# A search in place of a cyclic weight buffer, and all convolutions ahead of mixer B, in a two-layer conv/gMLP decoder step

## Chip, cores, metric

One Trainium2 chip, 8 cores. Each core runs the same program on one sequence of 2,048 rows and 16 sample rows. The metric is the device time of the slowest of the 8 cores, in microseconds. Some executions of any kernel on this chip fall into a slower state (one die at a lower granted clock, 1,483 to 1,730 us here); they are left out everywhere, and only fast runs are compared.

Names: PE is the TensorE matmul unit, DVE the VectorE, ACT the ScalarE, POOL the GpSimd engine (it issues all weight loads), SP the SyncE (it issues the other transfers).

## The reference, cut to what matters

Two layers; each is three token mixers side by side on one input projection, an output projection, and a SwiGLU FFN.

```python
def mixer(h, ...):
    z = h @ w_in
    a_val, a_gate, b_x, b_b, b_c, c_u, c_v = jnp.split(z, SPLITS, axis=-1)
    # A: GLU -> causal depthwise conv (31) -> LayerNorm over channels -> silu
    hist_a = jnp.concatenate([buf_a, a_val * jax.nn.sigmoid(a_gate)], axis=1)
    ya = jax.nn.silu(layernorm(causal_dwconv(hist_a, dw_a) + dw_a_bias, ln_a_g, ln_a_b))
    # B: b_b * conv_w3(b_c * b_x)
    yb = b_b * causal_dwconv(jnp.concatenate([buf_b, b_c * b_x], axis=1), conv_b_w)
    # C: u * (W_s_masked @ LN(v) + b), in chunks of 128 rows
    yc = jax.nn.gelu(c_u) * chunk_spatial(layernorm(jax.nn.gelu(c_v), ...), w_s, b_s)
    return jnp.concatenate([ya, yb, yc], axis=-1) @ w_o
# x += mixer(rmsnorm(x));  x += (silu(gate) * up) @ w_ffn_out;  two layers, one final norm
```

## The kernel before

The kernel records every operation as a node, and a list scheduler, run ahead of time, decides the order of each engine's queue. A node gets a due time, worked backwards from everything that waits for it, loads included. On each engine the ready node with the earliest due time goes next. And PE may run work up to 60 us ahead of the order in which the program states it.

```python
def place(self):
    for nd in reversed(nodes):
        d = nd.T if nd.e == "pe" else INF          # T: PE time before it in program order
        lat = 2000.0 + nd.nbytes / 200.0 if nd.nbytes else LAT
        for s, off in nd.succ:
            d = min(d, s.due + off - nd.cost - lat)
        # ... (cut)
    # ... take the engine that can start first; among its ready nodes:
            for nd in cand[e]:
                if self._ready(nd, base, free, e) <= s + 30.0:
                    d = nd.due
                    # ... (cut)
                    if pick is None or d < pick[0]:
                        pick = (d, nd)

AHEAD = 60000.0
BANKS_AHEAD = 4
```

All weights stream through one SBUF buffer of 26,624 bytes a partition. Places are handed out in a cycle. A load waits for every user of the earlier weights that it overwrites (`k.alias`).

```python
class Ring:
    def get(self, key):
        if key not in self.at:
            size, src = self.items[key]
            start = self.pos if self.pos + size <= RING else 0
            end = start + size
            hit = [v for v in self.live if v[0] < end and start < v[1]]
            assert all(v[3] in self.done for v in hit), (key, [v[3] for v in hit])
            b = Buf()
            self.k.alias([b], [v[2] for v in hit])
            # ... (cut: bookkeeping of what is left of the overwritten tenants)
            self.k.dma("pool", a, src, reads=self.hold.get(key, ()), writes=[b])
            self.at[key] = (a, b)
            self.pos = end
        return self.at[key]

# at the start, some loads are held until a piece of x has landed:
ring.hold = {("in", 0, 1): [b_x[0][3]], ("in", 0, 2): [b_x[7][3]], ("in", 0, 3): [b_x[7][1]],
             ("in", 0, 4): [b_x[7][2]], ("tp", 0, 0): [b_x[7][2]]}
```

Weights of a layer, by slot: in0 to in2 for mixer A; in3 and in4 for C; in5 to in7 for B's products (one each for j = 0, 1, 2); in8 and in9 for B's gate; tp0 to tp5 for the convolution, one for two conv units; o for the output projection. A slot of "in" takes 4,096 bytes (in9: 2,048), one of "tp" 5,120.

The mixer states its work in this order:

```python
for b in order:                                  # five blocks of rows
    unit_cu(0, b); unit_cu(1, b)                 # C: u
    for cp in range(8):
        if blk(2 * cp) == b:
            unit_cv(cp)                          # C: v, LayerNorm over tokens, spatial gate ("vtok")
    unit_b(0, b)                                 # B: product b_c * b_x for j = 0
    convs((0, 0, 1, 1, 2)[order.index(b)])       # A: conv units, 12 in all
unit_cs()
# ... (cut: sample rows)
ring.done.update([("in", l, 3), ("in", l, 4), ("in", l, 5)])
convs(2)
for j in (1, 2):
    for b in order:
        unit_b(j, b)
        convs(2 if j == 1 and b != order[4] else 0)
    ring.done.add(("in", l, 5 + j))
for b in range(5):
    unit_g(b)                                    # B: conv of width 3, gate
```

After the 12th conv unit follow LayerNorm statistics of mixer A, 24 passes on DVE, 24 SiLUs on ACT, 24 transfers back to channel order (`yaC`), and then x coming back for the residual add. The output projection needs all of these.

## Time and profile before

| kernel before | us |
|---|---|
| median of 4 runs at first | 1484.4 |
| median of the 35 fast runs taken with the experiments | 1486.1 (1479 to 1489) |
| slowest core / median core, over those runs | 1485.0 / 1477.8 |
| slowest minus fastest core | 10.9 |

The prediction shows the page and the stretches of the mixers. More views of the same trace are of core 1, which has a median span, in layer 1, and columns are: start, length, engine, line, operation, output<-inputs, count, and in brackets the idle time before the row and what ended it. First the queue of POOL, which issues the weight loads; these are the first three loads of convolution weights:

```profile
787.37 0.53 POOL L215 DMA_DIRECT2D ring<-w_tp  x1 [37.93 <-PE ps L514]
791.14 0.53 POOL L215 DMA_DIRECT2D ring<-w_tp  x1 [3.24 <-PE ps L514]
...
832.57 0.60 POOL L215 DMA_DIRECT2D ring<-w_tp  x1 [14.65 <-PE ps L514]
```

The third load comes 41 us after the second. POOL was released by a PE matmul: it waited until the weights that it was going to overwrite were no longer in use. PE:

```profile
801.21 0.41 PE L514 MATMUL ps<-WmT,vtok 128*64 128x128 bf16 x8 [2.01 <-DVE vtok L510]
801.56 3.49 PE L514 MATMUL ps<-hT,ring 128*128 128x512 bf16 x8
...
820.09 0.41 PE L514 MATMUL ps<-WmT,vtok 128*64 128x128 bf16 x8 [2.17 <-DVE vtok L510]
...
842.61 4.55 PE L514 MATMUL ps<-poly,ring 128*128 128x256 bf16 x40
```

PE stands idle for mixer C's LayerNorm on DVE ("vtok"), and the first convolutions (`ps<-poly,ring`) come only at 842.6, in a row of 40 matmuls. The order chosen ahead of time had put no other work into the gaps at 801 and 820. Last, what PE waited for between 745 and 1000 us (total, times, longest):

```profile
PE ps L514 <- DVE shr L502: 9.0, 1, 9.0
PE ps L514 <- DVE vtok L510: 5.6, 3, 2.2
```

The 9.0 us is the gap ahead of the output projection. No row names a weight load.

### The profile page before, as it was taken

How to read it: one execution, taken by the hardware profiler on the slowest of the kernel's cores; microseconds unless marked ns; L12 is line 12 of the kernel's file. 1: busy time of each engine (PE TensorE's matmuls, PEld its weight loads, DVE VectorE, ACT ScalarE, POOL GpSimd, SP SyncE). 2: the span in 40 equal slices, each digit the busy share in tenths (PEclk: the TensorE clock that was granted, in tenths of full speed). 3: DMA queues.
4: the chain of work that ended last, by engine and by line, in shares of the span. 5: the costliest groups of instructions: out<-in, count | busy, mean ns of one | idle time of the engine just before them, and what ended most of it. 6: DMA issues, size and time to landing. Idle time of an engine off the chain costs nothing.

```text
span 1480.5 us, 23695 instructions; the slowest of 8 cores (1475.1 to 1480.5 us)
## 1 busy us (share of the span) xinstructions
PE 1407.0 (95%) x8288; PEld 797.6 (54%) x8288; DVE 609.3 (41%) x1198; ACT 384.9 (26%) x742; POOL 78.6 (5%) x156
## 2 busy tenths in 40 slices
PE   3899989999999999999999988899999999999995
PEld 1446644655555555555456654365555555555553
DVE  2564787622223222223563569673222232222237
ACT  3533463411110011110242356333111001111114
POOL 0002100000000000000000210000000000000000
PEclk9899999999999999999999999899999999999998
DMA  9744761322122212223134275322413212122006
GB/s 208 188 74 67 118 151 22 58 44 36 33 40 43 43 30 43 33 38 53 57 87 87 37 113 83 92 36 39 71 20 59 43 29 40 32 44 37 14 0 230
DMA packets 51107, 95.28 MB, mean 64 GB/s; under 512 B 6256, under 2 KB 26256, under 8 KB 50960
## 3 DMA queue, kind: packets, MB, share of 16 engines
q0 software_dynamic: 16704, 56.63, 23.3%
q1 hardware_dynamic: 34288, 37.14, 9.3%
q8 instruction: 70, 1.15, 0.3%
q14 instruction: 45, 0.37, 0.1%
HBM read 132.22 MB, written 13.33 MB: 98 GB/s over the span
## 4 chain that ended last, share of the span: by engine, by line
PE 86%; DVE 4%; DMA 3%; issue 3%; ACT 2%; SPq 2%; POOL 0%; DVEq 0%; ACTq 0%; POOLq 0%
PE ps L514 86%; DMA xT<-x_in 2%; SPq L215 2%; DVE hT L502 1%; DVE shr L502 1%; ACT poly L484 1%; DVE xT L502 1%; DMA poly<-hist 0%; ACT shr L484 0%; DVE xT L499 0%; DVE vtok L510 0%; ACT shr L491 0%; DVE bnst L840 0%; DVE hT L499 0%; ACT L484 0%
## 5 line engine op out<-in xcount | busy, mean ns | idle before, releaser
L514 PE MATMUL ps<-hT,ring 128*128 128x512 bf16 (+3 forms) x5168 | 933.3, 339 | 20.0 <-DVE cvb L502 10.1
L514 PEld LDWEIGHTS ps<-hT,ring 128*128 128x128 bf16 x5168 | 506.5, 98 | 422.0 <-issue 34.2
L499 DVE TENSOR_TENSOR gT<-ps,fs 128x512 bf16<-128x512 f32 (+2 forms) x220 | 129.4, 588 | 478.7 <-PE ps L514 466.4
L514 PE MATMUL ps<-gT,ring 128*128 128x512 bf16 (+2 forms) x1760 | 311.8, 338 | 0.0
L484 ACT ACTIVATE fs<-ps 128x512 f32<-128x512 f32 (+2 forms) x220 | 113.1, 515 | 638.1 <-PE ps L514 599.3
L514 PEld LDWEIGHTS ps<-gT,ring 128*128 128x128 bf16 x1760 | 172.2, 98 | 135.1
L499 DVE TENSOR_TENSOR xT<-ps,xT 128x512 f32<-128x512 f32 (+2 forms) x240 | 140.0, 586 | 219.3 <-PE ps L514 218.5
L491 ACT ACTIVATE shr<-xT 128x512 bf16<-128x512 f32 (+2 forms) x179 | 92.5, 544 | 221.5 <-DVE xT L499 96.3
L502 DVE SCALAR_TENSOR_TENSOR hT<-xT,pD,shr 128x512 bf16<-128x512 f32 (+2 forms) x160 | 95.2, 641 | 12.4 <-ACT shr L484 12.4
L514 PE MATMUL ps<-shr,ones_b 128*128 128x512 bf16 (+2 forms) x200 | 51.7, 354 | 33.3 <-ACT shr L491 32.6
L499 DVE TENSOR_TENSOR hist<-ps,ev 128x512 bf16<-128x512 f32 (+1 forms) x60 | 34.7, 581 | 53.8 <-PE ps L514 41.0
L514 PE MATMUL ps<-yaC,ring 128*128 128x512 bf16 (+1 forms) x240 | 56.7, 342 | 0.0
L215 POOL DMA_DIRECT2D ring<-w_fi x44 | 23.2, 528 | 613.1 <-PE ps L514 613.1
L514 PEld LDWEIGHTS ps<-shr,ones_b 128*128 128x128 bf16 x200 | 19.7, 99 | 52.9 <-issue 39.4
L514 PE MATMUL ps<-u_t,ring 128*128 128x512 bf16 (+2 forms) x160 | 41.9, 344 | 0.0
L484 ACT ACT_TABLE_LOAD x26 | 33.4, 1283 | 26.2 <-PE ps L514 11.6
L492 DVE TENSOR_TENSOR shr<-xT 128x512 bf16<-128x512 f32 (+2 forms) x45 | 27.2, 624 | 28.5 <-DMA xT<-x_in 23.0
L502 DVE SCALAR_TENSOR_TENSOR shr<-hist,pAB,shr 128x512 f32<-128x512 bf16 (+1 forms) x60 | 36.1, 640 | 4.6 <-ACT shr L942 3.1
L514 PEld LDWEIGHTS ps<-yaC,ring 128*128 128x128 bf16 x240 | 23.7, 99 | 19.2 <-issue 1.7
L215 POOL DMA_DIRECT2D ring<-w_fo x32 | 16.9, 530 | 305.2 <-PE ps L514 302.9
L514 PE MATMUL ps<-ring,hT 128*128 128x256 bf16 (+1 forms) x272 | 32.4, 273 | 0.0
L499 DVE TENSOR_TENSOR xT<-xT,lnA 128x512 f32<-128x512 f32 x48 | 30.4, 682 | 1.2 <-ACT lnA L484 1.2
(85 smaller groups left out, 465.4 us busy)
## 6 DMA issues: line engine op xcount, KB each, us to landing
ring<-w_fi POOLq DMA_DIRECT2D x44, 512.0 KB, 5.6
ring<-w_fo POOLq DMA_DIRECT2D x32, 352.0 KB, 4.6
ring<-w_in POOLq DMA_DIRECT2D x18, 512.0 KB, 7.9
ring<-w_tp POOLq DMA_DIRECT2D x12, 640.0 KB, 8.0
xT<-x_in SPq DMA_DIRECT2D x6, 1024.0 KB, 21.2
y_out<-xT SPq DMA_DIRECT2D x6, 1024.0 KB, 5.4
ring<-w_o POOLq DMA_DIRECT2D x8, 512.0 KB, 6.9
poly<-hist SPq DMA_DIRECT2D x48, 64.0 KB, 3.3
```

What stands on the lines that cost most here:

```text
L215: fn = lambda eng: eng.dma_start(out=out, in_=in_)
L484: k.op("act", lambda e: e.activation(out=ap(out), in_=ap(in_), func=func, bias=bias, scale=scale), reads, writes, width(out), SETS.get(func))
L491: k.either({"act": lambda e: e.activation(out=out, in_=a, func=AF.Square), "dve": lambda e: e.tensor_tensor(out=out, in0=a, in1=a, op=ALU. ...
L492: "dve": lambda e: e.tensor_tensor(out=out, in0=a, in1=a, op=ALU.mult)}, reads, writes, width(out))
L499: k.op("dve", lambda e: e.tensor_tensor(out=ap(out), in0=ap(a), in1=ap(b), op=op), reads, writes, width(out))
L502: k.op("dve", lambda e: e.scalar_tensor_tensor(out=ap(out), in0=ap(in0), scalar=scalar, in1=ap(in1), op0=op0, op1=op1), reads, writes, wid ...
L514: k.node("pe", [((lambda e, p=p: e.matmul(ap(p[0]), lhsT=p[1], rhs=p[2], start=p[3], stop=p[4])), max(width(p[0]), 40) * 0.43, p[5] if len ...
```

## The change

The intent was to have mixer A's convolutions done before mixer B's work, so that B's projections cover A's LayerNorm chain; and to let weights take whichever place has been free longest, so that convolution weights can turn over beside live projection weights.

```diff
-class Ring:
+class Stream:
@@
+    def done(self, *keys):
+        for key in keys:
+            self.freed[key] = self.k.clock
     def get(self, key):
         if key not in self.at:
             size, src = self.items[key]
-            start = self.pos if self.pos + size <= RING else 0
+            best = None
+            for start in sorted({0} | {p for v in self.live for p in (v[0], v[1], v[0] - size, v[1] - size)}):
+                if start < 0 or start + size > RING:
+                    continue
+                hit = [v for v in self.live if v[0] < start + size and start < v[1]]
+                since = max([self.freed.get(v[3], 1e12) for v in hit], default=-1.0)
+                if best is None or since < best[0]:
+                    best = (since, start, hit)
+            assert best[0] < 1e12, (key, self.live)
+            _, start, hit = best
@@ (cut: all calls of ring.done.add become ring.done)
@@ the mixer (cut: the sample rows and the finer placing of convs in the first loop)
+            if l == 0:
+                for i, b in enumerate(order):
+                    unit_cu(0, b); unit_cu(1, b)
+                    for cp in range(8):
+                        if blk(2 * cp) == b:
+                            unit_cv(cp)
+                            convs(...)
+                unit_cs()
+                ring.done(("in", l, 3), ("in", l, 4))
+                convs(12)                        # all that are left
+                for j in range(3):
+                    for b in order:
+                        unit_b(j, b)
+                    ring.done(("in", l, 5 + j))
+            else:
+                # the same, but unit_b(0, b) stays in the first loop, and only
+                # unit_b(1, b) and unit_b(2, b) come after convs(12)
```

More of the change, by code (lines that the diff above doesn't have):

```diff
@@ L384, in __init__ @@
         self.items = items
-        self.pos = 0
         self.live = []
-        self.done = set()
+        self.freed = {}
         self.at = {}
         self.hold = {}
+    def done(self, *keys):
+        for key in keys:
+            self.freed[key] = self.k.clock
     def get(self, key):
@@ L393, in get @@
             size, src = self.items[key]
-            start = self.pos if self.pos + size <= RING else 0
+            best = None
[8 more added lines that the diff above has]
+            _, start, hit = best
             end = start + size
-            hit = [v for v in self.live if v[0] < end and start < v[1]]
-            assert all(v[3] in self.done for v in hit), (key, [v[3] for v in hit])
             b = Buf()
@@ L404, in get @@
             self.at[key] = (a, b)
-            self.pos = end
         return self.at[key]
@@ L538, in build_program @@
                     items[("fo", l, g, m)] = (NJG * 256, w_fo[l, g, m])
-        ring = Ring(k, ring_t, items)
+        ring = Stream(k, ring_t, items)
         def wcol(key, cols):
@@ L773, in unit_conv @@
                 if g2 % 2 == 1:
-                    ring.done.add(("tp", l, g2 // 2))
+                    ring.done(("tp", l, g2 // 2))
                 V = v32[:, 2 * g2:2 * g2 + 2, :]
@@ L979, in mixer @@
             for j in range(3):
-                ring.done.add(("in", l, j))
+                ring.done(("in", l, j))
             a_in()
@@ L992, in convs @@
                         unit_conv(conv.popleft())
-            for b in order:
-                unit_cu(0, b)
-                unit_cu(1, b)
-                for cp in range(8):
-                    if blk(2 * cp) == b:
-                        unit_cv(cp)
-                unit_b(0, b)
-                convs((0, 0, 1, 1, 2)[order.index(b)])
-            unit_cs()
-            for j in range(3):
-                sample_a(j)
-            sample_ln()
-            sample_stat()
-            ring.done.update([("in", l, 3), ("in", l, 4), ("in", l, 5)])
@@ L1008, in mixer @@
-            convs(2)
-            for j in (1, 2):
-                for b in order:
-                    unit_b(j, b)
-                    convs(2 if j == 1 and b != order[4] else 0)
-                    if j == 2 and b == SB:
-                        sample_b(0)
-                        sample_b(1)
-                        sample_b(2)
-                ring.done.add(("in", l, 5 + j))
+            if l == 0:
+                for i, b in enumerate(order):
+                    unit_cu(0, b)
+                    unit_cu(1, b)
+                    for cp in range(8):
+                        if blk(2 * cp) == b:
+                            unit_cv(cp)
+                            convs(((0, 0, 1, 3, 3) if l else (0, 0, 0, 3, 3))[i] if blk(2 * cp) != blk(2 * cp + 2) else 1 if i > (1 if l else 2) else 0)
+                unit_cs()
+                ring.done(("in", l, 3), ("in", l, 4))
+                convs(12)
+                for j in range(3):
+                    sample_a(j)
+                sample_ln()
+                sample_stat()
+                for j in range(3):
+                    for b in order:
+                        unit_b(j, b)
+                    ring.done(("in", l, 5 + j))
+                for j in range(3):
+                    sample_b(j)
+            else:
+                for i, b in enumerate(order):
+                    unit_cu(0, b)
+                    unit_cu(1, b)
+                    for cp in range(8):
+                        if blk(2 * cp) == b:
+                            unit_cv(cp)
+                            convs((0, 0, 1, 3, 3)[i] if blk(2 * cp) != blk(2 * cp + 2) else 1 if i > 1 else 0)
+                    unit_b(0, b)
+                unit_cs()
+                ring.done(("in", l, 3), ("in", l, 4), ("in", l, 5))
+                convs(12)
+                for j in range(3):
+                    sample_a(j)
+                sample_ln()
+                sample_stat()
+                for j in (1, 2):
+                    for b in order:
+                        unit_b(j, b)
+                    ring.done(("in", l, 5 + j))
+                for j in range(3):
+                    sample_b(j)
@@ L1021, in mixer @@
                 unit_g(b)
-            ring.done.update([("in", l, 8), ("in", l, 9)])
+            ring.done(("in", l, 8), ("in", l, 9))
             sample_silu()
@@ L1050, in mixer @@
                     if b == 4 and m % 2:
-                        ring.done.add(("o", l, m // 2))
+                        ring.done(("o", l, m // 2))
             k.retire(B.values())
@@ L1094, in ffn @@
                 for j in js[:head]:
-                    ring.done.add(("fi", l, j))
+                    ring.done(("fi", l, j))
                 for j in js[head:]:
@@ L1098, in ffn @@
                         unit_in(j, b)
-                    ring.done.add(("fi", l, j))
+                    ring.done(("fi", l, j))
                 last = g == JG - 1
@@ L1103, in ffn @@
                         unit_out(g, m, b)
-                    ring.done.add(("fo", l, g, m))
+                    ring.done(("fo", l, g, m))
                 if last:
@@ L1116, in ffn @@
                     for m in range(8 - TAIL, 8):
-                        ring.done.add(("fo", l, g, m))
+                        ring.done(("fo", l, g, m))
             for r_ in b_g:
```

## The prediction

> **What bounds the kernel now.** I read the summary of busy time first, then the stretches of the span, then what the TensorE (PE) waited for, then the timeline around the longest gaps. The summary, and PE's row and clock row of the 40 slices (37 us each):
>
> ```profile
> span 1480.5 us, 23695 instructions; the slowest of 8 cores (1475.1 to 1480.5 us)
> PE 1407.0 (95%) x8288; PEld 797.6 (54%) x8288; DVE 609.3 (41%) x1198; ACT 384.9 (26%) x742; POOL 78.6 (5%) x156
> ...
> PE   3899989999999999999999988899999999999995
> ...
> PEclk9899999999999999999999999899999999999998
> ```
>
> PE sets the time: only 1480.5 - 1407.0 = 73.5 us of it are gaps. The slices put them at the start, at the end, and in the mixers of layer 0 (slices 3 to 8) and layer 1 (21 to 26); both FFNs are full. The change touches neither start nor end, so the mixers' gaps are all that can be won. PE's waits, longest first:
>
> ```profile
> PE ps L514 <- ACT shr L491: 33.1, 11, 10.2
> PE ps L514 <- DVE cvb L502: 10.1, 1, 10.1
> PE ps L514 <- DVE vtok L510: 6.2, 5, 2.1
> PE ps L514 <- DMA xT<-x_in: 4.3, 1, 4.3
> ```
>
> The first is squares for the norm, nearly all at start and end (0.9 us of it lies in the two mixers after 100 us). The second and fourth are one place met twice: the start of the output projection, in layer 1 and layer 0. The stretches, cut at events that I found in the timeline (columns: length, busy us and instruction count of PE, PE weight load, DVE, ACT, POOL, then granted clock, DMA share, GB/s):
>
> ```profile
> 97.00:165.00 68.00, 66.16 (x522) 44.83 (x520) 40.25 (x114) 27.31 (x58) 12.20 (x25) 1.00 0.65 104
> ...
> 172.40:215.40 43.00, 37.81 (x209) 20.02 (x207) 36.46 (x61) 25.19 (x52) 2.11 (x4) 0.97 0.55 117
> ...
> 793.00:845.00 52.00, 46.40 (x328) 29.61 (x327) 24.08 (x71) 14.54 (x32) 6.46 (x14) 0.97 0.36 70
> 845.00:880.00 35.00, 31.28 (x255) 21.05 (x253) 21.55 (x58) 19.25 (x42) 7.49 (x14) 1.00 0.78 122
> 880.00:930.00 50.00, 38.96 (x234) 22.59 (x233) 44.91 (x84) 27.12 (x58) 2.11 (x4) 0.93 0.46 78
> ```
>
> Length less PE busy is the gap: 1.8, 5.2, 5.6, 3.7 and 11.0 us, 27.3 in all. The 5.2 and the 11.0 lie between the last convolution of mixer A and the first matmul of the output projection, and there DVE is busy 36.5 of 43 and 44.9 of 50 us. The timeline at the end of that stretch in layer 1:
>
> ```profile
> 916.20 1.89 DVE L499 TENSOR_TENSOR xT<-xT,lnA 128x512 f32<-128x512 f32 x3
> 917.04 3.06 ACT L484 ACTIVATE poly<-xT,pPP 128x256 bf16<-128x256 f32 x6 [1.45 <-DVE xT L499]
> ...
> 928.77 7.16 SPq L215 DMA_DIRECT2D xT<-xscr  x5
> 930.00 1.44 PE L514 MATMUL ps<-hT,ring 128*128 128x512 bf16 x3 [10.07 <-DVE cvb L502]
> ```
>
> So the chain is: last conv, LayerNorm statistics, 24 DVE passes, 24 SiLUs on ACT, 24 DMAs back to channel order, then the projection. Its last DVE pass comes only at 918, because DVE shares those 50 us with mixer B's gating. The wait named "DVE cvb" is only the DVE work that happened to end last; PE is out of work because all of mixer A's output is needed first. Nowhere in PE's list is a wait for weights.
>
> **What the Trainium skill says.** "Perfetto Trace Analysis", section Optimization Strategy: with regimes in which the most-contended engine changes, interleaving them can help. The trace agrees that this is such a case: DVE is at 90% in 880 to 930 and at 46% in 793 to 845. "TensorE: Matmul & The Clock Gate", What's actually happening: after an idle window of about 3.4 us PE runs at half clock until some 3.4 us of work have passed. The trace agrees: after the 10.07 us gap three 512-column matmuls took 1.44 us against 0.81 a little later, and 930 to 940 holds 39 matmuls where 940 to 950 holds 48. "DMA: Bandwidth & Descriptors", Issuing engines are not separate DMA queues: all queues share 16 engines, so bursts slow each other. The trace agrees: around the convs of layer 1 the weight loads come in a burst,
>
> ```profile
> ring<-w_tp POOLq DMA_DIRECT2D x3, 640.0 KB, 8.6
> ring<-w_in POOLq DMA_DIRECT2D x2, 512.0 KB, 13.7
> ```
>
> 13.7 us to landing there, 7.9 as the median of the run.
>
> **The change, part by part.**
>
> 1. Weight buffer. The cyclic buffer becomes a search for the place whose tenants were released earliest. No instruction is added or removed: same loads, same bytes. By itself about 0. It matters because the cycle could not skip a tenant still in use; with the search, conv weights (six loads of 5,120 B a partition) can turn over beside live projection weights (4,096 B each, 26,624 B in all).
>
> 2. Order. All 12 conv units of a layer now come before mixer B's later projections. Counting program order: before, the last conv stood ahead of 7 of B's 15 block units in both layers; after, ahead of all 15 in layer 0 (two 256-wide and three 512-wide blocks per j) and 10 in layer 1. A full-width B unit is 16 matmuls; at 95 matmuls in the 20 us from 240 that is 3.4 us, and one j of 2,064 columns 13.9 us. The gating adds 120 matmuls, 20.8 us. PE work between the last conv and the projection:
>  - layer 0: before 2 x 3.4 + 13.9 + 20.8 = 41.5 us, after 3 x 13.9 + 20.8 = 62.5;
>  - layer 1: before 3.4 + 13.9 + 20.8 = 38.1, after 2 x 13.9 + 20.8 = 48.6.
>  The chain took 43.0 and 50.0 us: more than PE had, by 1.5 and 11.9, near the gaps of 5.2 and 11.0 (PE had also run a little ahead).
>
> 3. The chain itself shortens where DVE is free. From layer 1's groups: 24 LayerNorm passes of 682 ns, 16.4 us; gating 18 x 748 + 12 x 479 ns + 9 x 685 + 6 x 416 = 27.9 us; B's products about 0.6 each. Once started before 10 B units, the passes meet only 6 us of B's products: 2.2 us of statistics + 16.4 + 6 + about 2 for the last SiLUs + 5 for the DMAs (918 to 923) + 9 for x coming back (206.9 to 215.4 in layer 0) = 41 us, below 48.6 and 62.5. Both gaps should close, with under 1 us left in layer 0 and about 2 in layer 1 (where 48.6 us of PE face 16.4 + 5.8 + 27.9 = 50 us of DVE; the projection, free to start, can fill in).
>
> 4. The cold clock after them goes too: 9 missing matmuls, 1.9 us, in layer 1; in layer 0 the first eight took 3.4 us instead of 1.7, 1.7 us.
>
> Sum of the win: (5.2 - 0.7 + 1.7) + (11.0 - 2 + 1.9) = 17.1 us.
>
> 5. Costs and the rest. Convs next to the token mixer C put more on DVE there: per pair of chunks about 4 us, per conv some 1.9 shared with ACT, against PE's 14 us per 512 block with four convs; below the bound, but these chains are short of slack. Layer 1's first two blocks keep their order, so the waits on vtok there (5.6 us of gaps in 793 to 845, and 8 matmuls at 0.43 us) should stay. The last six convs still come in one batch in layer 1 with three weight loads close behind: about 3 us of gap, as the 3.7 now. In layer 0 the first B weights used to be resident early and now arrive after six conv loads: 0 to 3 us. Together I charge 1 us.
>
> Net 16 us: 1484.4 - 16 = 1468 us.
>
> **The rivals.**
>  - The wait turns into one for weights: B's loads queue behind conv loads. For: landing up to 13.7 us in a burst, DMA share 1.0 at 140 to 160. Against: conv loads now spread over a longer stretch. It would give back 5 to 8 us: 1475.
>  - DVE becomes the bound: from the last conv to the end of the projection it has 50 us plus some 55 of residual adds and norm against PE's 104 in layer 1. For: that near balance. Against: norm can run on under the FFN, where DVE is idle 70%. The gap in layer 1 would halve only: 1474.
>  - The denser schedule also fills the vtok gaps, since convs are ready work for PE: up to 8 us more, 1460.
>  - No gain at all, if the order on the queues hardly moved, since they are scheduled ahead by readiness: 1484. Against: the conv start was tied to weights that could not be loaded before.
>
> **Range and chances.** Everything removable in the mixers is about 28 us of gaps and 5.3 of cold clock (3.6 above, 1.7 at 803), 33 us or 2.2%. Passing 2% needs 29.7 us, 90% of it: 5%. Slower by 2% would need a new stall of 30 us: 1%. Range: 25 us won, 1459, to 7 us won, 1477.
>
> **What would show it.** Step 2: statistics of mixer A start earlier, before most of B's products, and PE's waits on "DVE cvb" and on x coming back vanish or fall under 2 us. Step 3: LayerNorm passes done well before the gating ends. Step 4: clock 1.0 at the projection's start. Step 5: waits on vtok remain in layer 1. Wrong if a wait on weight loads above 3 us appears at B's first units, if vtok or conv casts cost PE clearly more than 9.4 us in layer 1, or if the gap before the projection stays.

## The result

| | before | after |
|---|---|---|
| median of the fast runs of that measurement, us | 1486.8 | 1458.1 |
| ratio after / before | | 0.9812, 95% interval 0.9796 to 0.9828 |
| second measurement of the ratio | | 0.9828, 0.9802 to 0.9855 |
| slowest / median core | 1485.0 / 1477.8 | 1456.9 / 1453.5 |
| slowest minus fastest core | 10.9 | 7.2 |

A ratio here is the mean time of one kernel's fast runs over the mean of the other's in the same rounds, so it isn't quite the ratio of the medians. The change won 28 us by the first measurement and some 25 by the second, against 16 predicted; 1458 lies one microsecond below the low end of the range. The page of the changed kernel (its slowest core; of these the first two lines, PE's row and the clock row of the 40 slices):

```profile
span 1457.8 us, 23609 instructions; the slowest of 8 cores (1449.7 to 1457.8 us)
...
PE 1392.4 (96%) x8174; PEld 797.1 (55%) x8288; DVE 610.5 (42%) x1201; ACT 382.9 (26%) x740; POOL 79.9 (5%) x156
...
PE   3899999999999999999998999999999999999995
...
PEclk8999999999999999999999999999999999999998
```

(On this core 114 matmul records are missing, so its PE time is not compared with before's.) Before, four of the mixers' slices had an 8 in PE's row (the 6th and the 24th to 26th), now one has (the 22nd), and the dip of the clock in the 26th is gone. The waits of PE on this core, to be held against the four rows in the prediction:

```profile
PE ps L523 <- ACT shr L500: 29.5, 10, 7.3
PE ps L523 <- DVE vtok L519: 5.0, 4, 2.0
...
PE ps L523 <- DMA xT<-xscr: 2.3, 1, 2.3
```

The 10.1 us ahead of the projection in layer 1 became 2.3 us of waiting for x itself. The first row, which lies at the start and the end of the program, reads 29.5 where the prediction's reads 33.1, though on another core.

To place the gain I cut each of the 8 traces at the same events and took the median of the cores (length, then PE's idle time in it, us):

| stretch | before | after |
|---|---|---|
| start to mixer A's rows leaving for the conv layout, layer 0 | 96.5, 28.2 | 89.6, 27.4 |
| to LayerNorm statistics | 72.9, 1.9 | 52.1, 4.1 |
| to the output projection | 45.5, 5.2 | 64.9, 0.9 |
| to the FFN | 69.4, 0.3 | 68.3, 0.3 |
| start to FFN of layer 0 | 283.7 | 274.3 |
| conv layout to LayerNorm statistics, layer 1 | 88.9, 9.4 | 74.3, 5.2 |
| to the output projection | 52.5, 9.9 | 52.0, 2.2 |
| to the FFN | 68.8, 0.4 | 69.0, 0.4 |
| end of FFN of layer 0 to FFN of layer 1 | 249.9 | 235.1 |

The two FFNs take 463.1 and 461.8 us in both kernels. Since work moves between stretches, and a matmul at half clock counts as busy, a second account is fairer: from the first matmul on, the sum over matmuls of the time to the start of the next one, less its columns at 2.4 per ns (the full clock according to the Trainium skill, "TensorE: Matmul & The Clock Gate", What's actually happening; the trace agrees: a warm 512-column matmul took 0.216 us here, 1.73 us between the starts of two groups of eight). That is idle time and slow clock together. It fell by 6.0 us at the start (33.4 to 27.4), by 4.0 in the rest of layer 0 (14.3 to 10.4) and by 14.1 in layer 1 (28.4 to 14.4), 24 of the 25 us by which the median core got faster between the two traces. (A recount with slightly other cuts gave 34.5 to 27.8, 15.1 to 11.7 and 30.2 to 16.0, also 24.) The remaining few of the 28 us are the slowest core coming nearer to the median.

Layer 1 again on core 1, weight loads first, then PE:

```profile
778.48 0.54 POOL L215 DMA_DIRECT2D ring<-w_tp  x1 [1.25 <-PE ps L523]
780.33 0.54 POOL L215 DMA_DIRECT2D ring<-w_tp  x1 [1.31 <-PE ps L523]
...
798.61 0.70 POOL L215 DMA_DIRECT2D ring<-w_tp  x1 [5.66 <-PE ps L523]
```

```profile
790.47 0.41 PE L523 MATMUL ps<-WmT,vtok 128*64 128x128 bf16 x8 [2.00 <-DVE vtok L519]
...
795.70 2.36 PE L523 MATMUL ps<-poly,ring 128*128 128x256 bf16 x20
...
902.26 0.81 PE L523 MATMUL ps<-hT,ring 128*128 128x512 bf16 x3 [2.21 <-DMA xT<-xscr]
```

The third load now follows the second by 18 us instead of 41. The first convolutions run at 795.7, among mixer C's units, where before they came after them; counted from the end of the first FFN that is 58 us instead of 94. The projection starts after a gap of 2.2 us and, on this core, at full clock (three 512-column matmuls in 0.81 us).

One more difference shows at the very start. Before (core 7), then after (core 7), the first weight loads:

```profile
1.56 1.20 POOL L215 DMA_DIRECT2D ring<-w_in  x2 [0.87 <-POOLq L410]
```

```profile
1.56 0.67 POOL L215 DMA_DIRECT2D ring<-w_in  x1 [0.88 <-POOLq L419]
```

Before, two loads of 512 KB went out at once beside the loads of x: in0, which mixer A needs first, and in5, which only mixer B's units use. The convolutions' order in layer 0 gives in5's place to tp0, which is held until x has come, so in5's early load vanishes. As a side effect that the intent doesn't mention, x lands sooner: over the cores, the median of the last landing is 51.5 us before and 46.4 after.

After I had read this, two candidates stood: the order of the work (with the start's lighter traffic), which I believed, and the freer loads that the search alone makes possible.

### The profile page after: what moved, and what is told of

Read it like the earlier page. It is cut to its first block, busy times and chain, and to the rows that moved or that the text cites. A ratio compares the mean times of both kernels' runs of the same rounds, so it can differ in the third digit from the quotient of the medians.

```text
span 1457.8 us, 23609 instructions; the slowest of 8 cores (1449.7 to 1457.8 us)
## 1 busy us (share of the span) xinstructions
PE 1392.4 (96%) x8174; PEld 797.1 (55%) x8288; DVE 610.5 (42%) x1201; ACT 382.9 (26%) x740; POOL 79.9 (5%) x156
## 4 chain that ended last, share of the span: by engine, by line
PE 87%; DVE 4%; DMA 3%; issue 3%; ACT 2%; SPq 1%; POOL 0%; DVEq 0%; ACTq 0%; POOLq 0%
PE ps L523 87%; DMA xT<-x_in 2%; DVE hT L511 1%; DMA poly<-hist 1%; DMA xT<-xscr 1%; SPq L215 1%; ACT poly L493 1%; DVE xT L511 1%; DVE shr L511 0%; ACT shr L493 0%; DVE bnst L849 0%; DVE xT L508 0%; ACT shr L500 0%; DVE vtok L519 0%; POOL rs L855 0%
## 5 line engine op out<-in xcount | busy, mean ns | idle before, releaser
L523 PE MATMUL ps<-hT,ring 128*128 128x512 bf16 (+3 forms) x5092 | 918.1, 337 | 8.9 <-DMA xT<-xscr 2.3
L523 PE MATMUL ps<-shr,ones_b 128*128 128x512 bf16 (+2 forms) x194 | 50.8, 353 | 34.5 <-ACT shr L500 29.3
L523 PE MATMUL ps<-poly,ring 128*128 128x256 bf16 x240 | 29.8, 277 | 2.8 <-DMA poly<-hist 2.8
```

What stands on the lines that cost most here:

```text
L523: k.node("pe", [((lambda e, p=p: e.matmul(ap(p[0]), lhsT=p[1], rhs=p[2], start=p[3], stop=p[4])), max(width(p[0]), 40) * 0.43, p[5] if len ...
```

## Experiments

All kernels gave correct results. Those named together ran on the same chip and share its runs of the kernel before: the first four together, the next four, then the last but one three; the last kernel ran with its own runs of before.

| run | what it is | median us | ratio to before, 95% interval | slowest / median core | spread |
|---|---|---|---|---|---|
| e1_alloc_only | search, old order | 1465.0 | 0.9857, 0.9831–0.9882 | 1463.8 / 1455.0 | 12.0 |
| e2_layer1_new | search, new order in layer 1 alone | 1475.7 | 0.9916, 0.9889–0.9944 | 1474.5 / 1465.7 | 12.0 |
| e3_layer0_new | search, new order in layer 0 alone | 1457.0 | 0.9806, 0.9780–0.9832 | 1455.9 / 1451.6 | 8.2 |
| e4_before_hold | before, in5 held | 1477.0 | 0.9937, 0.9912–0.9962 | 1475.8 / 1473.4 | 5.5 |
| e5_extra_load | after, one more 512 KB at the start | 1462.2 | 0.9849, 0.9829–0.9869 | 1461.1 / 1458.1 | 7.7 |
| e6_old_waits | e1 with the cycle's waits added | 1489.9 | 1.0034, 1.0015–1.0053 | 1488.8 / 1482.6 | 11.1 |
| e7_alloc_and_hold | e1, in5 held | 1455.0 | 0.9802, 0.9782–0.9822 | 1453.9 / 1451.6 | 5.4 |
| e8_both_layer0 | after, layer 1 in layer 0's order | 1470.6 | 0.9903, 0.9886–0.9920 | 1469.5 / 1465.6 | 7.6 |
| e9_hold_two | e7, in9 held (faulty) | 1473.9 | 0.9925, 0.9901–0.9948 | 1472.8 / 1469.4 | 6.4 |
| e10_after_again | after | 1459.7 | 0.9828, 0.9802–0.9855 | 1458.6 / 1453.2 | 9.3 |
| e11_e7_again | e7 | 1456.4 | 0.9807, 0.9783–0.9830 | 1455.3 / 1451.8 | 5.5 |
| e12_hold_two_mended | e7, in9 held until all of x has come | 1454.5 | 0.9794, 0.9775–0.9813 | 1453.5 / 1450.4 | 6.0 |

### The search alone, and each layer's order

The edit of the first is to keep the new buffer and put the mixer's loop back as it was; of the next two, to do so in one layer only.

```diff
 class Stream:                 # as in the change
@@ e1: the mixer's loop of the kernel before, with
-            ring.done.update([("in", l, 3), ("in", l, 4), ("in", l, 5)])
+            ring.done(("in", l, 3), ("in", l, 4), ("in", l, 5))
@@ e2: that loop for l == 0, the change's loop for l == 1
@@ e3: the change's loop for l == 0, that loop for l == 1
```

> The new weight buffer with the old order of units in both layers. Theory (the gain is the order of units, plus one weight load of mixer B that no longer runs at the very start; here it still does): the time stays at before, ratio 0.996 to 1.003, some 1480 to 1488 us, and the gaps before both output projections stay above 4 us (layer 0) and 8 us (layer 1). Rival 1 (freer placement of weights is itself the gain): ratio 0.985 or lower, 1465 us.

> New buffer, old order in layer 0, new order in layer 1. Theory: layer 1 gives its 14 us and no more, ratio 0.990 to 0.992, about 1471 us; layer 0 and the start lose nothing and gain nothing. Rival 1: as the full change, 0.981. Rival 2 (layer 1's part comes from what layer 0 left in the buffer): 0.996 or more.

> New buffer, new order in layer 0, old order in layer 1. Theory: 6 us at the start and 4 in layer 0's mixer, ratio 0.992 to 0.995, about 1476 us; layer 1 keeps its gap of about 10 us before the projection. My prediction on record would have had only 6 us in layer 0 and none at the start: 0.996. Rival 1: 0.981.

My theory was that the search alone would be worth about nothing. It fell with the first run: the search alone takes 21 us off (1486 times 0.0143), with the program's order unchanged. Counted as in the second account above (the recount), e1 loses as much at the start as the kernel before, 34.5 us, but 4.4 us less in the rest of layer 0 and 16.5 less in layer 1. Adding the new order in layer 1 makes it 10 us slower (e2), and removing it from the full change costs nothing (e3). That e2 lies within the range of my theory for it (0.990 to 0.992) is luck: the theory had this order win 14 us, and against e1 it loses. What PE waited for in layer 1 with the search alone, on core 1 in the same window as above:

```profile
PE ps L523 <- DVE vtok L519: 3.5, 3, 2.0
PE ps L523 <- DMA xT<-xscr: 1.8, 1, 1.8
```

The 9.0 us ahead of the projection is gone, as in the full change. And the third load of convolution weights, and PE:

```profile
817.57 0.60 POOL L215 DMA_DIRECT2D ring<-w_tp  x1 [2.58 <-PE ps L523]
```

```profile
813.79 1.26 PE L523 MATMUL ps<-poly,ring 128*128 128x256 bf16 x10
```

Convolutions run among mixer C's units at 814, though the program states their order exactly as before. (Core 1 is this run's slowest; from the end of the first FFN it is 63 us, against 94 before.) The last conv ends 111 us after the first FFN, against 126 before. The buffer's own bookkeeping says why; these are the places in layer 1 and whose users each load must wait for:

| load | cycle (before) | search (e1) |
|---|---|---|
| tp2 | over in3 and in2 | over tp0 |
| in6 | over in4 and in3 | over tp1 |
| tp3 | over in5 and in4 | over in0 and in5 |
| tp4 | over tp0 and in5 | over in3 and in0 |

The cycle put tp2 over in3, the weights of C's `u`, which are in use until C ends. The scheduler's own plan (its clock, not the chip's) for the first half of some conv units in layer 1 shows both ways in which this acts:

| conv unit | before: due / ready / placed | search: due / ready / placed |
|---|---|---|
| 0 | 771.6 / 816.0 / 854.9 | 761.8 / 820.7 / 825.5 |
| 4 | 780.5 / 853.9 / 860.2 | 772.6 / 841.6 / 852.6 |
| 8 | 782.4 / 871.1 / 871.1 | 782.4 / 862.2 / 863.0 |
| 10 | 783.3 / 882.9 / 883.4 | 783.3 / 868.8 / 869.1 |

Units 4 to 11 become ready 9 to 14 us earlier, since their weights load earlier. Unit 0 was ready early in both, but with the search the load of tp2 waits for it, which makes it due 10 us earlier and so puts it 29 us earlier.

What e2's layer-1 order costs is only partly settled. Its layer 1 has 7.9 us of idle PE between LayerNorm statistics and projection against 2.2 after. On core 1 PE's list shows 3.5 us of that as waits for mixer B's gating on DVE, and 4.0 us, right ahead of the projection, without a releaser. The timeline shows a gating pass on DVE that ends 0.1 us before PE starts:

```profile
914.93 0.68 DVE L508 TENSOR_TENSOR hT<-ps,shr 128x512 bf16<-128x512 f32 x1
...
915.74 1.44 PE L523 MATMUL ps<-hT,ring 128*128 128x512 bf16 x3 [3.98 <-issue]
```

Cores 0 and 6 show the same 0.1 us. So DVE, still gating, is the likely reason (the prediction's second rival); this is read from the times and was not tested. In e2 the places that layer 0 leaves behind differ from those in the full change, so the same program order gives other waits (in6 goes over in3 and in0, and waits for C; after, it goes to a place that is free by then). I didn't separate this from the order itself.

### The old waits put back

```diff
+RING_WAITS = {('tp', 0, 0): [('in', 0, 0), ('in', 0, 1)], ...,
+              ('tp', 1, 2): [('in', 1, 3), ('in', 1, 2)], ('in', 1, 6): [('in', 1, 4), ('in', 1, 3)], ...}
@@ in get(), on top of e1
             self.k.alias([b], [v[2] for v in hit])
+            for x in RING_WAITS.get(key, ()):
+                self.k.alias([b], [self.at[x][1]])
```

The places stay those of the search; every load of tp, and of in6 to in9, also waits for the weights that it would have overwritten in the cycle.

> The kernel of the first run (new buffer, old order of units), with one thing put back: each load of conv weights and of mixer B's later weights waits for the same earlier weights as in the kernel before, although it is written to another place. New theory (the buffer's gain is that these loads no longer wait for weights that stay in use, so that the convs are ready earlier): all 22 us come back, ratio 0.997 to 1.003, layer 1 at 249 to 251 us between the end of one FFN and the start of the next. Rival (the places themselves, or fewer pieces of free space, matter): it stays near 0.986, layer 1 near 233 us.

All of the gain is gone, and 5 us more (1.0034, slightly above what was expected). In layer 1 PE stands again before the projection (core 1, same window):

```profile
PE ps L528 <- DVE hT L513: 11.7, 2, 10.8
PE ps L528 <- DVE shr L510: 4.1, 1, 4.1
PE ps L528 <- DVE vtok L524: 4.0, 3, 2.0
```

So what the search buys is the waits that it doesn't make, not the places themselves. The run has old and new waits together, so it is a bit stricter than the kernel before, which fits the 5 us. It also tells the two ways apart a little: its first convolutions still run early, at 816 us, because their due time stays the early one, yet the gain is lost. What counts, as far as this run can tell, is when the later weights may load, so when the last conv is done (127 us after the first FFN, 126 before, 111 in e1).

### The early load at the start

```diff
@@ e4 (on before) and e7 (on e1): B's first weights wait for x as the others do
-    ("in", 0, 4): [b_x[7][2]], ("tp", 0, 0): [b_x[7][2]]}
+    ("in", 0, 4): [b_x[7][2]], ("tp", 0, 0): [b_x[7][2]], ("in", 0, 5): [b_x[7][2]]}
@@ e5 (on after): a load that the scheduler doesn't know of, into a place not yet in use;
@@ a later load waits for it. The order of all other instructions is unchanged
+            if e == "pool" and nd.nbytes and wn == 1:
+                eng.dma_start(out=self.extra[0], in_=self.extra[1]).then_inc(self.extra[2].h, 16)
```

> The kernel before with one entry more: the first load of mixer B's weights waits until x has landed, as the first conv weights do. Theory (that load, 512 KB in the first microseconds beside the loads of x, costs the start): 6 us less until mixer A's last unit of layer 0, ratio 0.994 to 0.997, 1476 to 1480 us. Rival 3 (the start gained because the new order of units puts other work between mixer A's units): no gain, ratio 0.999 to 1.001.

> The changed kernel with one 512 KB load of mixer B's weights added right behind the first weight load, into a place not yet used, and unknown to the scheduler, so that no instruction changes its place. Theory (the traffic beside the loads of x is what costs the start): the slowest core loses 4 to 9 us, ratio to before 0.984 to 0.988, and the spans of the cores spread by 10 us or more in place of 7. Rival (only the order that the scheduler made of it costs): no change, 0.981, spread 7.

Holding in5 alone, with the cycle and the old order, takes 9 us off the slowest core (1485.0 to 1475.8) and 4 off the median core. The reverse test is cleaner because no order changes: one more 512 KB load at 2 us costs the full change 3 to 5 us (0.9849 against 0.9812 and 0.9828, and its interval overlaps the second's), and 4.6 to 4.9 on the median core. Its time came as expected; its spread did not, 7.7 us where I had expected 10 or more. The moment at which x is complete can be read from one row, since the setup transfers are held until then. Core 7, of before, after and e5 in this order:

```profile
52.14 0.34 SPq L215 DMA_DIRECT2D poly<-p_ws  x1
```

```profile
46.01 0.34 SPq L215 DMA_DIRECT2D poly<-p_ws  x1
```

```profile
51.21 0.34 SPq L215 DMA_DIRECT2D poly<-p_ws  x1
```

Over the cores the median landing of the last piece of x is 51.5, 46.4 and 50.8 us; a second trace of the changed kernel (e10) has 47.6. How far the cores drift apart goes with the early load in most runs (10.9 to 12.0 us with it in before, e1, e2 and e6; 5.4 to 9.3 without), but e5 has it and 7.7, so I don't call that shown.

### Search and hold together, without any new order

> The new buffer and the held first load of mixer B's weights, with the old order of units in both layers. New theory (freer loads give 22 us, the held load some 8 us of the slowest core, the order of units nothing of its own): ratio 0.979 to 0.983, 1456 to 1462 us, as the full change. Rival (the new order is needed for the last 6 to 8 us): as the first run, 0.985 to 0.987, 1465 us.

This is the decisive run: none of the reordering, and it is as fast as the full change (0.9802 and, repeated, 0.9807, against 0.9812 and 0.9828). In the call that ran both it was ahead by 3 us, 1456.4 against 1459.7. The repeats:

> The changed kernel once more, on the same chip as the other two: 0.981 within 0.002, 1456 to 1460 us.

> The new buffer with the old order and one held load once more, on the same chip. Theory: equal to the changed kernel or up to 4 us below it, 0.979 to 0.981.

### More of the new order

```diff
-            if l == 0:
+            if True:             # and the other branch removed
```

> The changed kernel with layer 1 in the order of layer 0 (all of mixer B's units after the convs). If an earlier end of the convs still were worth something, layer 1 would lose its wait for x coming back (2.2 us): ratio 0.979 to 0.980. If the order has no gain of its own once the loads are free: 0.981 within 0.002.

Layer 1 in the order of layer 0 has LayerNorm statistics still earlier (67.1 us after the conv layout, against 74.3) but loses it all afterwards: 72.8 us to the projection with 8.3 us of idle PE. The expectation missed. On core 1 between 840 and 930 us:

```profile
PE ps L523 <- issue: 3.8, 1, 3.8
PE ps L523 <- ACT ev L504: 3.4, 2, 2.7
```

B's products need their PSUM results copied out by ACT and DVE (`ev`), and those engines are now busy with LayerNorm and SiLU of mixer A at that very time. That this is the reason was not tested. The 3.8 us without a releaser end, as in e2, with a gating pass on DVE (from 916.69 for 0.68 us; PE starts at 917.36).

### The next early load, and a version at least as fast as both

In e7 the search gives in9, of 256 KB, a place that was never used, so its load could also go out at once.

```diff
@@ e9, on e7
+    ("in", 0, 9): [b_x[7][2]]}
@@ e12, on e7: at the point where x_all (all of x landed) is defined
+    ring.hold[("in", 0, 9)] = [x_all]
```

> The new buffer, the old order of units, and both early loads of mixer B's weights (512 KB, and 256 KB of its last slot, which the freer buffer also starts at once) held until x has landed. Theory (traffic beside x costs the start): the last load of x lands at 46 to 48 us in place of 50, and the time falls 2 to 4 us below the kernel with one held load: ratio 0.977 to 0.979, about 1452 us, and below the changed kernel. Rival (the one load was all that mattered): 0.980.

> The run with two held loads, mended: the second load now waits for the first arrival of x alone, not for its return after mixer A. Theory (traffic beside x costs the start; the 20 us lost before were PE waiting for that load): the last load of x lands at 46 to 49 us, layer 0's projection stage is back at 51 to 52 us, and the time is 1452 to 1455 us, ratio 0.977 to 0.980. Rival (the one load was all that mattered): 1456, 0.981.

The first try was a mistake of mine, and the trace shows it. The hold is looked up where the program first asks for in9, and by then `b_x[7][2]` stands for x's second arrival, ahead of the projection. So in9 came at 199 us (core 1, POOL's queue, then PE's list for 80 to 285 us):

```profile
199.00 0.53 POOL L215 DMA_DIRECT2D ring<-w_in  x1 [16.82 <-DMA xT<-x_in]
```

```profile
PE ps L523 <- DMA ring<-w_in: 14.3, 1, 14.3
```

Here, for once, PE's list names a weight load, and the run is 17 us slower (1473.9 against 1456.4). Mended, the kernel takes 1454.5 us, 0.9794 of before: the fastest here. Since 0.9802 and 0.9807 of e7 lie within its interval, the 2 us between them are likely but not shown.

## Why the prediction was right or wrong

Right, and confirmed by the changed trace:

- PE sets the time, the FFNs have nothing to give, and the mixers' gaps are the prize. The gaps ahead of the projection closed, 5.2 to 0.9 and 9.9 to 2.2 us (steps 2 and 3 had "under 1" and "about 2"). Their cold clock (step 4) went in layer 0: over the 8 us behind the gap, matmuls took 1.8 us beyond full clock before and 0.1 after, in the median core. In layer 1 it went on half of the cores only: 2.2 us before; after, 0.1 on cores 0, 1, 6 and 7 and 1.8 on cores 2 to 5, though the gaps are alike (2.1 to 2.3 us).
- No wait for weight loads appeared (first rival), and DVE did not become the bound in this form of the change (second rival; in e2 and e8 it seems to).
- The direction and the class as far as they are settled: the result lies at the 2% line, 0.9812 with an interval that reaches 0.9796, and 0.9828 the second time. The size was too small, 16 us against 28 or 25.

Wrong:

- **Part 1, the buffer: "By itself about 0".** This is the step that failed. By itself it is worth 21 us, and with the waits put back nothing. I counted instructions and bytes and concluded that nothing changes; but in a kernel whose order is computed from readiness and due time, the list of whom a load waits for is an input to the order of everything. The working had the clue in its last rival: "the conv start was tied to weights that could not be loaded before". I used it to argue for the new order, where it was an argument for the buffer.
- **Part 2, the order, as the cause.** The closing of the gaps was credited to B's units standing after the convolutions in the program. With the old order and the search they close just as well (2.2 and 2.0 us in e1), and with the new order in layer 1 alone they don't (7.9 us in e2). Right was that statistics of mixer A must start earlier against B's products; wrong was what makes them.
- **"The change touches neither start nor end".** The start gained 6 to 7 us in the median core. I had the place of in5 at hand, and step 5 even notes that B's first weights "used to be resident early and now arrive after six conv loads", but charges it as a cost of 0 to 3 us. It was a gain, because the load it removes competed with x.
- **Step 5, the conv batch.** I left 5.6 us of vtok gaps in layer 1 and added a conv batch of 3. The vtok gaps did stay, 4.0 us in the median core. What went is the waiting in the conv batch: its statistics matmuls waited 3.8 us for DVE and ACT (`shr`) before, and 1.1 after. So the stage from the conv layout to the statistics lost 9.4 us of PE's idle time before and 5.2 after, and its accounted loss, with the cold clock, fell from 14.6 to 9.2 us. The third rival ("also fills the vtok gaps ... up to 8 us more, 1460") came true for 1.6 us; that its 1460 is near the result is luck. In layer 0 the same stage went the other way, 5.0 to 7.7, which is the cost that step 5 sized as 1 us.
- **Step 3, the chain at 41 us.** From statistics to the projection layer 1 took 52.5 us before and 52.0 after: the chain hardly shortened. What closed the gap is that PE had enough work for it. (A small slip in step 2: one j of B is 13.7 us from its own 3.4, not 13.9; nothing hangs on it.)

The sum by what was measured, in the median core: start 6.0, layer 0 elsewhere 6.6 for its projection less 2.6 for its conv stage, layer 1 8.7 for its projection and 5.4 for its conv stage, together 24, against 17.1 less 1. The two projection terms, 15.3 us, are near the 17.1 predicted. That is luck in part, since what closed the gaps is the search, which part 1 had put at 0. What was missing is the start and the conv stage of layer 1, and the slowest core's own gain.

## What to carry to other kernels

Where an order is computed ahead of time, ask of every buffer rule what it makes wait and whom: a load that must wait for weights in use delays ready work without ever showing as a wait for weights, so look at the gaps between loads in the issuing queue. A change of two parts is to be measured part by part before either is credited; here the visible half, the reordering, was worth nothing that these runs could tell beyond the load it happened to remove. And look at what goes out in the first microseconds beside the data that everything waits for.

## What the Trainium skill lacked or had wrong

- "Perfetto Trace Analysis", section Optimization Strategy, says to find the gaps on the bounding engine and what ends them, and that bubbles that recur can mean too little SBUF for the next tile. Here PE's gaps in layer 1 named DVE, no row there named a weight load, and the size of the buffer was enough: with the same 26,624 bytes, another rule of reuse took 21 us off (e1), and the old waits took it back (e6). No page says that a reuse rule can bound an engine in this hidden way, or that the issuing queue is where it shows (41 us between two loads before, 18 after).
- "DMA: Bandwidth & Descriptors", section Issuing engines are not separate DMA queues, says that all transfers share 16 engines. The runs agree and give the size: 512 KB from POOL's queue beside x on SP's delayed the last of x by 3 to 4 us (50.8 in the median core against 47.6 and 46.4) and the end by 3 to 5 (e5). The prediction's two lines on bursts are both of POOL's own queue, so they show a burst in one queue and not this sharing.
- "TensorE: Matmul & The Clock Gate", section Seeing it yourself, says to expect 13/16 of the clock in all-core dense matmul. In the fast runs all eight cores had a mean granted clock of 0.98 to 0.995 while PE was 95% busy. Lower ones stand only in the slow runs that are left out, on one die: 0.94 (1531 us, the changed kernel), and down to 0.82 (1730 us, the kernel before), which is close to 13/16. The same page names an idle window of about 3.4 us for the half clock, in the section that the prediction cites; after the 2.01 us gap at 801 us of the kernel before, eight 512-column matmuls took 3.49 us, where eight take 1.89 at full clock. The length of the gap alone doesn't decide it: behind gaps of 2.1 to 2.3 us ahead of the changed kernel's projection in layer 1, four cores lost 1.8 us this way and four 0.1.
